# Early final norm in three places, old rows gathered ahead of both write-backs, last row scale on the sums

## Chip, cores and metric

One core of a Trainium2 chip runs the kernel. The metric is device time in microseconds (us) of one execution. The engines are TensorE (PE; its weight loads are PEld), VectorE (DVE), ScalarE (ACT), GpSimd (POOL) and SyncE (SP), whose queue issues most DMAs.

## What is computed

A layer over 2048 latent tokens of 1024 channels: a mixing sub-layer (convolution and mLSTM), then a channel sub-layer in which each of 16 experts picks its 256 tokens, then a final RMS norm. The change touches the end of this:

```python
def rmsnorm(x, g):
    xf = x.astype(jnp.float32)
    y = xf * lax.rsqrt(jnp.mean(xf * xf, axis=-1, keepdims=True) + EPS)
    return (y * g.astype(jnp.float32)).astype(x.dtype)

# one expert e: idx are its tokens, g their router weights
a = jnp.einsum('ecd,edf->ecf', xe, w_gate)
u = jnp.einsum('ecd,edf->ecf', xe, w_up)
ye = jnp.einsum('ecf,efd->ecd', jax.nn.silu(a) * u, w_down) * g[..., None]
...
xl = xl + ml[5] * expert_choice_moe(hl, w_router[layer], w_gate_e[layer], w_up_e[layer], w_down_e[layer])
return rmsnorm(xl, g_final)
```

ml[5] is a row of 1024 factors, the same for all tokens; in the kernel it is `ml5b`, and g_final is `gfb`.

## The kernel before

The experts run one after the other, e from 0 to 15. An expert's 1408 hidden channels are 11 tiles of 128, taken in six pairs (`pr` 0 to 5, the last with one tile). For each pair SP loads a tile of w_gate, of w_up (`load_w`, line 85) and of w_down (`wsplit_d`, line 1068). All products are made from a high and a low part: ScalarE copies the raw weights to the high part (line 92 `whi`, line 1074 `dhi`), VectorE subtracts it from the raw ones (line 96 `wlo`, line 1076 `dlo`). TensorE then does three matmuls for each product: lines 1173 to 1175 for gate and up (into `psx`), 1109 to 1111 for down (into four accumulators `ac`, two row halves by two column halves). The raw gate and up tiles have two buffers, their split parts three each, the w_down parts two.

After gate and up, ScalarE applies silu (1177), VectorE multiplies (1178), and the result is split again into `hh` (ScalarE, 1180) and `hl` (VectorE, 1182). The down product of a pair comes one pair later (`pend`), behind the gate and up matmuls of the next pair. When an expert's last pair is through, `finish` scales the sums by the token weight and ml5b (1128) and writes the rows to the tensor ACC in DRAM with an indirect DMA of GpSimd: experts 0 to 13 with an accumulating write (1133). Expert 14 gathers the old rows (1125), adds them (1131), writes (1135), norms the rows (squares, `rsqrt` on GpSimd in lines 80 and 81, lines 1138 and 1139) and scatters them to `out` (1140). Expert 15 does the same at the end (lines 1210 to 1231), but its w_down tiles have been multiplied by ml5b on GpSimd (line 1070), so that its sums need the token weight alone. 

In the last two experts the final norm of all 2048 rows is also computed early, in 16 tiles of 128 rows (`early`): load from ACC by SP (1092), square and row sum on ScalarE (1085), two small steps on GpSimd, scaling on VectorE (1095), store to `out` by SP (1096). Rows that experts 14 and 15 chose are overwritten by their scatters later. Expert 14 does two tiles in each pair from `pr` 1 on (tiles 0 to 9), expert 15 two in each of `pr` 1 to 3. Tiles with an even number use the buffer `ea` (one slot), the others `yv` (two slots), which the write-backs use too. The squares themselves are not needed; they go to a tile `eq` in the slot with the tag `oh`, of which there is one.

The rows of the next expert are fetched in `pr` 1 (`xgather`: a one-hot tile `oh` made by VectorE in line 1008, 16 matmuls into `pi`, line 1012, two gathers into the two slots `gx`, line 1018), and in `pr` 3 (`xprep`) TensorE transposes them (1052) and ScalarE and VectorE turn them into the high and low parts `xh` and `xl` (1055, 1060, 1061). The old rows of lines 1125 and 1213 use the slots `gx` as well.

The order on each engine and queue is set by a planner, which places each instruction when its inputs are there by its own estimate of times and takes what is earlier in the program first. On the chip every engine then runs its list in that order and waits where an input is not there.

Of the kernel before, what the change touches and what calls it, by code (L numbers as in the profile page):

```python
# [8 lines left out]
F32 = mybir.dt.float32  # L9
F32R = mybir.dt.float32r  # L10
BF16 = mybir.dt.bfloat16
I32 = mybir.dt.int32
I16 = mybir.dt.int16
AF = mybir.ActivationFunctionType
ALU = mybir.AluOpType
# [4 lines left out]
P = 128  # L20
# [18 lines left out]
def kernel(ctx, tc, x, c, cx, c_ctx, w_mod, b_mod, g_norm1, g_norm2, w_in, w_out, conv_w, conv_b,  # L39
# [956 lines left out]
    with tc.tile_pool(name="xw", bufs=2, reuse_waits="tile") as xraw, tc.tile_pool(name="xh", bufs=2, reuse_waits="tile") as xhi, \  # L996
# [67 lines left out]
        def wsplit_d(src, rows, gate=None, after=None, col=None):  # L1064
            raw = xraw.tile([P, rows, D], F32, name="draw", tag="draw")
            if gate is not None:
                V.tensor_copy(raw[:, 0, 0:1], gate)
            nc.sync.dma_start(raw, src)
            if col is not None:
                G.tensor_mul(raw, raw, col.unsqueeze(1).to_broadcast([P, rows, D]))  # L1070
            hi = xhi.tile([P, rows, D], F32R, name="dhi", tag="dhi")
            if after is not None:
                S.activation(hi[:, 0, 0:1], after, AF.Copy)
            S.activation(hi, raw, AF.Copy)  # L1074
            lo = xhi.tile([P, rows, D], F32R, name="dlo", tag="dlo")
            V.tensor_sub(lo, raw, hi.bitcast(F32))  # L1076
            return hi, lo
# [12 lines left out]
        def early(t):  # L1090
            a = wk.tile([P, D], F32, name="ea", tag="yv" if t % 2 else "ea", bufs=2 if t % 2 else 1)
            nc.sync.dma_start(a, ACC[t * P:(t + 1) * P, :])
            q = wk.tile([P, D], BF16, name="eq", tag="oh", bufs=1)
            fr = rms(a, q)
            V.scalar_tensor_tensor(a, a, fr, gfb, op0=ALU.mult, op1=ALU.mult)  # L1095
            nc.sync.dma_start(out[t * P:(t + 1) * P, :], a)
# [16 lines left out]
        def rows(e, hf_):  # L1113
            return bass.IndirectOffsetOnAxis(ap=idx_of[e][:, hf_:hf_ + 1], axis=0)

        idx_of = {}

        def finish(e, xp, accs, hfs=(0, 1)):
            gg = xp[2]
            idx_of[e] = xp[3]  # L1120
            for hf_ in hfs:
                yv = wk.tile([P, D], F32, name="yv", bufs=2)
                if e == NE - 2:
                    ar = wk.tile([P, XW], F32, name="gx", bufs=2)[:, :D]
                    G.indirect_dma_start(out=ar, out_offset=None, in_=ACC, in_offset=rows(e, hf_))
# [10 lines left out]
                q = wk.tile([P, D], BF16, name="eq", tag="oh", bufs=1)  # L1136
                fr = rms(yv, q)
# [5 lines left out]
        pend = []  # L1143
        for e in range(NE):
            xh, xl, gg, idx = xp
            accs = None
            nxt = None
            for pr in range(npair):
# [3 lines left out]
                for src in (w_gate_e, w_up_e):  # L1152
# [5 lines left out]
                    else:  # L1158
# [3 lines left out]
                              xl.bitcast(F32)[:, KD - 1, 0:1] if e == 0 and pr < 2 else None,  # L1162
                              ml5b if e == NE - 1 else None)
                if e == 0 and pr == 0:
                    other_places(xl.bitcast(F32)[:, KD - 1, 0:1])
                hts = []
# [17 lines left out]
                last = pr == npair - 1  # L1184
                if pend and not (e == NE - 1 and last):
# [9 lines left out]
                if e >= NE - 2 and pr:  # L1195
                    cuts = ((0, 2, 4, 6, 8, 10), (10, 12, 14, 16, 16, 16))[e - NE + 2]
                    for t in range(cuts[pr - 1], cuts[pr]):
                        early(t)
# [7 lines left out]
        idx_of[NE - 1] = xp[3]  # L1206
        with tc.manual_schedule(engines={mybir.EngineType.PE}):
            (_, _, _, p1, _), (_, _, _, p2, _) = pend
            order = [[(p1, 0, 0), (p1, 0, 1), (p2, 0, 0)], [(p2, 0, 1)], [(p1, 1, 0), (p1, 1, 1), (p2, 1, 0)], [(p2, 1, 1)]]
            for hf_ in range(2):  # L1210
# [3 lines left out]
                q = wk.tile([P, D], BF16, name="eq", tag="oh", bufs=1)  # L1214
                fs = wk.tile([P, 2], F32, name="fs2", bufs=2)
                fr = wk.tile([P, 2], F32, name="fr2", bufs=2)
                for cc in range(2):
                    sl = slice(cc * 512, (cc + 1) * 512)
                    for pp, h_, c_ in order[hf_ * 2 + cc]:
                        down(accs, pp, (h_,), (c_,))  # L1220
                    V.scalar_tensor_tensor(yv[:, sl], accs[hf_ * 2 + cc], xp[2][:, hf_:hf_ + 1], ar[:, sl],
                                           op0=ALU.mult, op1=ALU.add)
                    S.activation(q[:, sl], yv[:, sl], AF.Square, accum_out=fs[:, cc:cc + 1])
# [33 lines left out]
```

## Time and profile before

| | |
|---|---|
| time, median of 3 runs | 2733.11 us (2732.84 to 2739.49) |
| the profiled execution | 2732.62 us |
| its span, first to last instruction | 2730.7 us |
| busy: PE, DVE, ACT, POOL | 2635.4, 1598.7, 1153.0, 338.0 us |
| mean granted TensorE clock | 0.987 of full speed |
| moved by DMA | 524.58 MB, mean 192 GB/s |

The profile is of one execution. A matmul's start is as recorded and its end is modelled. In a list of waits, the arrow names what the waiting instruction was released by. In a timeline, the text in brackets is the idle time of the engine in front of the instruction and its releaser; merged instructions have a count (x2). The granted clock is given as a share of full speed.

### The profile page before, as it was taken

The numbers are of one execution on the slowest core, as the hardware profiler recorded it, in microseconds if no ns is written. First come the engines' busy times: TensorE is split into PE (matmuls) and PEld (weight loads), VectorE is DVE, ScalarE is ACT, GpSimd is POOL, SyncE is SP. The second block draws the span as 40 slices with busy tenths as digits, with TensorE's granted clock in tenths as the row PEclk, the third lists the DMA queues.
The fourth block names the chain that finished last, engine by engine and source line by source line (L and its number), as shares of the span: only waits on it lengthen the run. The fifth ranks groups of instructions, "written<-read, shape, count | busy, mean of one in ns | idle before, by whom it ended". The sixth has DMA issues, their size and how long they took to land. (4 is left out here: it accounts for less than half of the span.)

```text
span 2730.7 us, 42905 instructions
## 1 busy us (share of the span) xinstructions
PE 2635.4 (97%) x17569; PEld 2371.4 (87%) x17570; DVE 1598.7 (59%) x2566; ACT 1153.0 (42%) x1707; POOL 338.0 (12%) x351
## 2 busy tenths in 40 slices
PE   8999999999999999499999999999999999999988
PEld 4988888888878888389999999999999999999877
DVE  5356455553576665666556656655665665566585
ACT  3243333422534343354444444444444444444443
POOL 1010000000111111210011001101100110110353
PEclk9999999999999999799999999999999999999999
DMA  8444554545656564176666666666766675675865
GB/s 268 136 145 157 171 161 145 186 127 165 213 190 198 181 211 156 40 247 206 197 208 217 189 205 208 212 201 198 222 191 205 203 218 196 194 234 183 277 233 192
DMA packets 382533, 524.58 MB, mean 192 GB/s; under 512 B 15072, under 2 KB 322736, under 8 KB 380288
## 3 DMA queue, kind: packets, MB, share of 16 engines
q1 hardware_dynamic: 327968, 437.96, 49.8%
q10 hardware_dynamic: 43792, 46.55, 5.0%
q0 software_dynamic: 10576, 37.32, 4.9%
q8 instruction: 138, 2.26, 0.3%
q14 instruction: 59, 0.48, 0.1%
HBM read 449.05 MB, written 72.61 MB: 191 GB/s over the span
## 5 line engine op out<-in xcount | busy, mean ns | idle before, releaser
L1174 PE MATMUL psx<-xl,whi 128*128 128x256 f32 x2816 | 786.9, 280 | 4.0 <-DVE xl L1061 4.0
L1173 PE MATMUL psx<-xh,whi 128*128 128x256 f32 x2816 | 788.8, 281 | 1.4 <-ACT whi L92 1.4
L1175 PE MATMUL psx<-xh,wlo 128*128 128x256 f32 x2816 | 787.8, 280 | 0.6 <-DVE wlo L96 0.6
L96 DVE TENSOR_TENSOR wlo<-wraw,whi 128x2048 fp32r<-128x2048 f32 x248 | 539.8, 2187 | 308.1 <-ACT whi L92 305.0
L92 ACT ACTIVATE whi<-wraw 128x2048 fp32r<-128x2048 f32 x248 | 447.1, 1805 | 374.4 <-PE psx L1174 121.3
L1174 PEld LDWEIGHTS psx<-xl,whi 128*128 128x128 f32 x2816 | 530.7, 188 | 7.0 <-DVE xl L1061 4.6
L1173 PEld LDWEIGHTS psx<-xh,whi 128*128 128x128 f32 x2816 | 530.2, 189 | 4.3 <-ACT whi L92 1.6
L1175 PEld LDWEIGHTS psx<-xh,wlo 128*128 128x128 f32 x2816 | 530.7, 189 | 1.4 <-DVE wlo L96 1.3
L1111 PE MATMUL ac<-dhi,hl 128*128 128x512 f32 x704 | 277.7, 396 | 4.4 <-DVE hl L1182 4.4
L1109 PE MATMUL ac<-dhi,hh 128*128 128x512 f32 x704 | 280.3, 398 | 0.0
L1110 PE MATMUL ac<-dlo,hh 128*128 128x512 f32 x704 | 279.0, 396 | 0.0
L1076 DVE TENSOR_TENSOR dlo<-draw,dhi 128x2048 fp32r<-128x2048 f32 x96 | 202.9, 2113 | 115.1 <-ACT dhi L1074 115.1
L417 PE MATMUL ps<-hlo,whi 128*128 128x512 f32 (+1 forms) x672 | 259.9, 387 | 0.0
L418 PE MATMUL ps<-hhi,wlo 128*128 128x512 f32 (+1 forms) x672 | 259.6, 387 | 0.0
L416 PE MATMUL ps<-hhi,whi 128*128 128x512 f32 (+1 forms) x672 | 259.2, 388 | 0.0
L1133 POOL DMA_INDIRECT ACC<-yv,idx x28 | 82.8, 2958 | 1135.4 <-DVE yv L1128 1024.2
L1074 ACT ACTIVATE dhi<-draw 128x2048 fp32r<-128x2048 f32 x96 | 170.2, 1772 | 74.7 <-PE ac L1111 72.5
L1180 ACT ACTIVATE hh<-sgt 128x256 fp32r<-128x256 f32 x176 | 73.2, 417 | 276.2 <-DVE sgt L1178 276.2
L1111 PEld LDWEIGHTS ac<-dhi,hl 128*128 128x128 f32 x704 | 132.4, 188 | 36.4 <-DVE hl L1182 4.6
L1177 ACT ACTIVATE sgt<-psx 128x256 f32<-128x256 f32 x176 | 65.5, 373 | 230.3 <-PE psx L1175 230.2
L1110 PEld LDWEIGHTS ac<-dlo,hh 128*128 128x128 f32 x704 | 132.8, 189 | 26.9
L1109 PEld LDWEIGHTS ac<-dhi,hh 128*128 128x128 f32 x704 | 132.5, 188 | 27.1
(410 smaller groups left out, 3984.7 us busy)
## 6 DMA issues: line engine op xcount, KB each, us to landing
wraw<-in_w_gate_e_dram SPq DMA_DIRECT2D x80, 1024.0 KB, 7.3
wraw<-in_w_up_e_dram SPq DMA_DIRECT2D x80, 1024.0 KB, 5.5
draw<-in_w_down_e_dram SPq DMA_DIRECT2D x80, 1024.0 KB, 5.1
wraw<-in_w_in_dram SPq DMA_DIRECT2D x56, 1024.0 KB, 5.5
pk<-PK SPq DMA_DIRECT2D x16, 1284.0 KB, 7.0
xt<-in_x_dram SPq DMA_DIRECT2D x32, 512.0 KB, 4.9
wraw<-in_w_mod_dram SPq DMA_DIRECT2D x16, 1024.0 KB, 10.5
wm<-in_w_mod_dram SPq DMA_DIRECT2D x8, 1024.0 KB, 9.5
```

The lines of the kernel that those rows point to most:

```text
L92: S.activation(hi, raw, AF.Copy)
L96: V.tensor_sub(lo, raw, hi.bitcast(F32))
L416: T.matmul(ps[:, :ntok], wh, his[k], start=k == 0, stop=False)
L417: T.matmul(ps[:, :ntok], wh, los[k], start=False, stop=False)
L418: T.matmul(ps[:, :ntok], lo[:, k, i * P:(i + 1) * P], his[k], start=False, stop=k == KD - 1)
L1076: V.tensor_sub(lo, raw, hi.bitcast(F32))
L1109: T.matmul(ac, hhs, dh[:, i, sl], start=f == 0, stop=False)
L1110: T.matmul(ac, hhs, dl[:, i, sl], start=False, stop=False)
L1111: T.matmul(ac, hls, dh[:, i, sl], start=False, stop=f == NFT - 1)
L1173: T.matmul(ps[:, m_], wh, xh[:, k], start=k == 0, stop=False)
L1174: T.matmul(ps[:, m_], wh, xl[:, k], start=False, stop=False)
L1175: T.matmul(ps[:, m_], lo[:, k, i * P:(i + 1) * P], xh[:, k], start=False, stop=k == KD - 1)
```

## The change

- `early` is cut in three. `early_load` issues the load, now behind the weight loads of its pair and ahead of the pair's matmuls. `early_scale` does the square, row sum and GpSimd steps, behind the pair's last `hh`: a copy of one element of `hh` into the scrap tile ties it there. `early_store` does the scaling and the store, in the next pair behind its weight loads.
- The scrap output of the squares is a view of `ghb`, a constant whose contents aren't needed any more, and no longer a tile in the slot `oh`.
- The old rows of expert 14 are gathered for both halves in `old_rows`, at the end of its last pair; before, each half's gather stood in `finish`.
- For expert 15, the multiplication of w_down by ml5b is gone. The sums are scaled by the token weight and ml5b in one step, and the old rows are added in a second.

```diff
@@ -1061,13 +1061,11 @@
                     V.tensor_sub(xl[:, k], xf, xh.bitcast(F32)[:, k])
             return xh, xl, gg, idx
 
-        def wsplit_d(src, rows, gate=None, after=None, col=None):
+        def wsplit_d(src, rows, gate=None, after=None):
             raw = xraw.tile([P, rows, D], F32, name="draw", tag="draw")
             if gate is not None:
                 V.tensor_copy(raw[:, 0, 0:1], gate)
             nc.sync.dma_start(raw, src)
-            if col is not None:
-                G.tensor_mul(raw, raw, col.unsqueeze(1).to_broadcast([P, rows, D]))
             hi = xhi.tile([P, rows, D], F32R, name="dhi", tag="dhi")
             if after is not None:
                 S.activation(hi[:, 0, 0:1], after, AF.Copy)
@@ -1087,11 +1085,18 @@
             rsqrt(fr, fs, 1.0 / D, 1)
             return fr
 
-        def early(t):
+        sq = ghb.bitcast(BF16)
+
+        def early_load(t):
             a = wk.tile([P, D], F32, name="ea", tag="yv" if t % 2 else "ea", bufs=2 if t % 2 else 1)
             nc.sync.dma_start(a, ACC[t * P:(t + 1) * P, :])
-            q = wk.tile([P, D], BF16, name="eq", tag="oh", bufs=1)
-            fr = rms(a, q)
+            return [t, a]
+
+        def early_scale(rec, behind):
+            S.activation(sq[:, 0:1], behind, AF.Copy)
+            rec.append(rms(rec[1], sq))
+
+        def early_store(t, a, fr):
             V.scalar_tensor_tensor(a, a, fr, gfb, op0=ALU.mult, op1=ALU.mult)
             nc.sync.dma_start(out[t * P:(t + 1) * P, :], a)
 
@@ -1115,14 +1120,20 @@
 
         idx_of = {}
 
+        def old_rows(e):
+            for hf_ in range(2):
+                ar = wk.tile([P, XW], F32, name="gx", bufs=2)[:, :D]
+                G.indirect_dma_start(out=ar, out_offset=None, in_=ACC, in_offset=rows(e, hf_))
+                old.append(ar)
+
+        old = []
+
         def finish(e, xp, accs, hfs=(0, 1)):
             gg = xp[2]
-            idx_of[e] = xp[3]
             for hf_ in hfs:
                 yv = wk.tile([P, D], F32, name="yv", bufs=2)
                 if e == NE - 2:
-                    ar = wk.tile([P, XW], F32, name="gx", bufs=2)[:, :D]
-                    G.indirect_dma_start(out=ar, out_offset=None, in_=ACC, in_offset=rows(e, hf_))
+                    ar = old[hf_]
                 for cc in range(2):
                     sl = slice(cc * 512, (cc + 1) * 512)
                     V.scalar_tensor_tensor(yv[:, sl], accs[hf_ * 2 + cc], gg[:, hf_:hf_ + 1], ml5b[:, sl],
@@ -1133,16 +1144,16 @@
                     G.indirect_dma_start(out=ACC, out_offset=rows(e, hf_), in_=yv, in_offset=None, compute_op=ALU.add)
                     continue
                 G.indirect_dma_start(out=ACC, out_offset=rows(e, hf_), in_=yv, in_offset=None)
-                q = wk.tile([P, D], BF16, name="eq", tag="oh", bufs=1)
-                fr = rms(yv, q)
+                fr = rms(yv, sq)
                 V.tensor_mul(ar, yv, gfb)
                 V.tensor_scalar(ar, ar, fr, None, op0=ALU.mult)
                 G.indirect_dma_start(out=out, out_offset=rows(e, hf_), in_=ar, in_offset=None)
 
         xp = xprep(0, xgather(0))
-        pend = []
+        pend, held = [], []
         for e in range(NE):
             xh, xl, gg, idx = xp
+            idx_of[e] = idx
             accs = None
             nxt = None
             for pr in range(npair):
@@ -1159,10 +1170,15 @@
                         ws.append(split_w(raw, KD, n * P))
                 dw = wsplit_d(w_down_e[0, e][f0 * P:(f0 + n) * P, :].rearrange("(i p) n -> p i n", p=P), n,
                               gg[:, 0:1] if e == 0 and pr < 2 else None,
-                              xl.bitcast(F32)[:, KD - 1, 0:1] if e == 0 and pr < 2 else None,
-                              ml5b if e == NE - 1 else None)
+                              xl.bitcast(F32)[:, KD - 1, 0:1] if e == 0 and pr < 2 else None)
                 if e == 0 and pr == 0:
                     other_places(xl.bitcast(F32)[:, KD - 1, 0:1])
+                for rec in held:
+                    early_store(*rec)
+                held = []
+                if e >= NE - 2 and pr:
+                    cuts = ((0, 2, 4, 6, 8, 10), (10, 12, 14, 16, 16, 16))[e - NE + 2]
+                    held = [early_load(t) for t in range(cuts[pr - 1], cuts[pr])]
                 hts = []
                 for i in range(n):
                     ps = pmm.tile([P, 2, 2 * P], F32, name="psx", tag="mm")
@@ -1182,6 +1198,8 @@
                     V.tensor_sub(hl, sgt, hh.bitcast(F32))
                     hts.append((hh, hl))
                 last = pr == npair - 1
+                for rec in held:
+                    early_scale(rec, hts[-1][0].bitcast(F32)[:, 0:1])
                 if pend and not (e == NE - 1 and last):
                     pe, pxp, paccs, ppr, plast = pend.pop()
                     if paccs is None:
@@ -1192,10 +1210,8 @@
                     else:
                         accs = paccs
                 pend.append((e, xp, accs, ([f0 + i for i in range(n)], hts, dw), last))
-                if e >= NE - 2 and pr:
-                    cuts = ((0, 2, 4, 6, 8, 10), (10, 12, 14, 16, 16, 16))[e - NE + 2]
-                    for t in range(cuts[pr - 1], cuts[pr]):
-                        early(t)
+                if e == NE - 2 and last:
+                    old_rows(e)
                 if pr == 1 and e + 1 < NE:
                     gth = xgather(e + 1)
                 if pr == 3 and e + 1 < NE:
@@ -1203,7 +1219,6 @@
             if nxt is not None:
                 xp = nxt
         accs = pend[0][2]
-        idx_of[NE - 1] = xp[3]
         with tc.manual_schedule(engines={mybir.EngineType.PE}):
             (_, _, _, p1, _), (_, _, _, p2, _) = pend
             order = [[(p1, 0, 0), (p1, 0, 1), (p2, 0, 0)], [(p2, 0, 1)], [(p1, 1, 0), (p1, 1, 1), (p2, 1, 0)], [(p2, 1, 1)]]
@@ -1211,16 +1226,16 @@
                 yv = wk.tile([P, D], F32, name="yv", bufs=2)
                 ar = wk.tile([P, XW], F32, name="gx", bufs=2)[:, :D]
                 G.indirect_dma_start(out=ar, out_offset=None, in_=ACC, in_offset=rows(NE - 1, hf_))
-                q = wk.tile([P, D], BF16, name="eq", tag="oh", bufs=1)
                 fs = wk.tile([P, 2], F32, name="fs2", bufs=2)
                 fr = wk.tile([P, 2], F32, name="fr2", bufs=2)
                 for cc in range(2):
                     sl = slice(cc * 512, (cc + 1) * 512)
                     for pp, h_, c_ in order[hf_ * 2 + cc]:
                         down(accs, pp, (h_,), (c_,))
-                    V.scalar_tensor_tensor(yv[:, sl], accs[hf_ * 2 + cc], xp[2][:, hf_:hf_ + 1], ar[:, sl],
-                                           op0=ALU.mult, op1=ALU.add)
-                    S.activation(q[:, sl], yv[:, sl], AF.Square, accum_out=fs[:, cc:cc + 1])
+                    V.scalar_tensor_tensor(yv[:, sl], accs[hf_ * 2 + cc], xp[2][:, hf_:hf_ + 1], ml5b[:, sl],
+                                           op0=ALU.mult, op1=ALU.mult)
+                    V.tensor_add(yv[:, sl], yv[:, sl], ar[:, sl])
+                    S.activation(sq[:, sl], yv[:, sl], AF.Square, accum_out=fs[:, cc:cc + 1])
                     V.tensor_mul(ar[:, sl], yv[:, sl], gfb[:, sl])
                     G.tensor_scalar(fr[:, cc:cc + 1], fs[:, cc:cc + 1], 1.0 / D, fr[:, 0:1] if cc else EPS,
                                     op0=ALU.mult, op1=ALU.add)
```

## Rows read from the trace of the kernel before

**Rows 1.** Profile page, part 5: VectorE's split of line 96 over the whole span.

```profile
L96 DVE TENSOR_TENSOR wlo<-wraw,whi 128x2048 fp32r<-128x2048 f32 x248 | 539.8, 2187 | 308.1 <-ACT whi L92 305.0
```

**Rows 2.** Windows: us, busy us (instructions) per engine, TensorE clock, DMA share, GB/s.

```profile
2335.00:2431.00 96.00, 96.00 (x700) 89.69 (x700) 57.41 (x64) 44.55 (x49) 8.59 (x4) 1.00 0.65 206
2529.00:2626.00 97.00, 83.29 (x564) 76.98 (x563) 66.58 (x65) 44.38 (x59) 30.82 (x26) 0.95 0.80 276
2626.00:2731.00 105.00, 86.80 (x592) 79.31 (x591) 64.39 (x60) 41.41 (x61) 49.27 (x35) 0.94 0.56 191
```

**Rows 3.** Waits of TensorE, 2400 to 2735: us in total, times, longest.

```profile
PE pi L1012 <- DVE oh L1008: 5.4, 1, 5.4
PE ptx L1052 <- DVE xf L1060: 5.2, 1, 5.2
PE ac L1111 <- DVE hl L1182: 4.4, 1, 4.4
PE psx L1174 <- DVE xl L1061: 3.1, 1, 3.1
PE psx L1175 <- DVE wlo L96: 0.6, 2, 0.3
```

**Rows 4.** Windows right behind three of the waits, columns as before.

```profile
2543.85:2548.50 4.65, 4.65 (x25) 4.65 (x24) 3.79 (x5) 0.80 (x2) 1.12 (x2) 0.50 1.05 377
2601.13:2603.10 1.97, 1.97 (x11) 1.97 (x10) 1.23 (x1) 0.06 (x1) 0.00 (x0) 0.50 1.03 383
2646.82:2651.00 4.18, 4.18 (x11) 3.32 (x12) 2.70 (x3) 2.41 (x4) 1.19 (x2) 0.59 0.77 221
```

**Rows 5.** Timelines of VectorE and GpSimd: start, us, engine, line, operation [idle before].

```profile
2587.56 1.28 DVE L1095 SCALAR_TENSOR_TENSOR ea<-ea,fr,ml2b 128x1024 f32<-128x1024 f32 x1 [0.44 <-POOL fr L81]
...
2589.50 4.63 POOL L1070 TENSOR_TENSOR draw<-draw,ml5b 128x2048 f32<-128x2048 f32 x1
...
2589.56 5.65 DVE L1095 SCALAR_TENSOR_TENSOR ea<-ea,fr,ml2b 128x1024 f32<-128x1024 f32 x1 [0.72 <-POOL fr L81]
...
2608.98 6.49 POOL L1070 TENSOR_TENSOR draw<-draw,ml5b 128x2048 f32<-128x2048 f32 x1 [1.49 <-DVE ea L1095]
...
2611.39 6.23 DVE L96 TENSOR_TENSOR wlo<-wraw,whi 128x2048 fp32r<-128x2048 f32 x1
...
2638.83 5.07 DVE L1139 TENSOR_SCALAR gx<-gx,fr 128x1024 f32<-128x1024 f32 x1 [1.83 <-POOL fr L81]
...
2663.36 0.75 DVE L1139 TENSOR_SCALAR gx<-gx,fr 128x1024 f32<-128x1024 f32 x1 [1.47 <-POOL fr L81]
```

**Rows 6.** Timelines of ScalarE and VectorE around the first wait.

```profile
2538.24 1.06 ACT L1085 ACTIVATE eq<-ea 128x1024 bf16<-128x1024 f32 x1 [8.71 <-DMA ea<-ACC]
...
2540.70 0.40 ACT L1180 ACTIVATE hh<-sgt 128x256 fp32r<-128x256 f32 x1
...
2541.57 1.22 DVE L1008 TENSOR_TENSOR oh<-ix,UA 128x2048 bf16<-128x2048 bf16 x1
```

**Rows 7.** Timeline of SP's queue: issues of loads.

```profile
2522.13 0.37 SPq L1068 DMA_DIRECT2D draw<-in_w_down_e_dram  x1
2534.62 1.29 SPq L1092 DMA_DIRECT2D ea<-ACC  x3
2536.00 0.38 SPq L85 DMA_DIRECT2D wraw<-in_w_up_e_dram  x1
```

**Rows 8.** Timelines of GpSimd and VectorE: second half row write-back of expert 14.

```profile
2647.34 0.98 POOL L1125 DMA_INDIRECT gx<-ACC,idx  x1 [0.30 <-issue]
...
2656.92 1.29 DVE L1131 TENSOR_TENSOR yv<-yv,gx 128x512 f32<-128x512 f32 x2
```

**Rows 9.** Timelines of VectorE and ScalarE: second half, last expert.

```profile
2717.13 1.45 DVE L1221 SCALAR_TENSOR_TENSOR yv<-ac,gg,gx 128x512 f32<-128x512 f32 x2 [0.26 <-PE ac L1111]
...
2718.61 0.63 ACT L1223 ACTIVATE eq<-yv 128x512 bf16<-128x512 f32 x1
```

**Rows 10.** Page, part 6: issues, KB each, median us to landing.

```profile
wraw<-in_w_gate_e_dram SPq DMA_DIRECT2D x80, 1024.0 KB, 7.3
```

## What the change does to the time

> **What bounds the kernel now.** I read the stages first [rows 2]. A middle expert keeps TensorE busy for all of its 96.00 us at granted clock 1.00, so there nothing but matmul work counts, and the diff does not touch it. The last two experts hold the holes: 83.29 busy of 97.00 us and 86.80 of 105.00, at clocks 0.95 and 0.94. The DMA share is 0.80 and 0.56 there, so the transfers as a whole do not bound these stages, though single bursts may.
>
> Next, TensorE's own list of waits [rows 3]: five entries, 5.4, 5.2, 4.4, 3.1 and 0.6 us, together 18.7, and all of them end on VectorE. Idling has an after-cost: right after three of the waits the granted clock is 0.50, 0.50 and 0.59, that is at or near the lower level of 1.2 GHz, for 4.65, 1.97 and 4.18 us [rows 4]. At the upper level (2.4 GHz, clock 1.00) the work of these stretches takes 2.3, 1.0 and 1.7 us less, 5.0 in all. So 18.7 + 5.0 = 23.7 us is what the last two experts lose, and nearly all that a change here can win.
>
> Then who makes VectorE late. Three of the waits have one cause [rows 5]. At 2589.50 GpSimd starts its multiplication of a w_down tile (line 1070, 4.63 us); the row scaling of line 1095 that starts on VectorE at 2589.56 takes 5.65 us instead of 1.28 and ends just after it. The same holds for the split of line 96 at 2611.39, inside the 6.49 us of the next multiplication (6.23 instead of a mean of 2.19 [rows 1]), and for line 1139 at 2638.83 (5.07 instead of 0.75). The two engines did not share here: VectorE stood still until GpSimd was done.
>
> The first wait is of another kind [rows 6]. The one-hot tile of line 1008 is what TensorE waits for; it is written on VectorE only at 2541.57. Its buffer (tag "oh", one slot) also serves as scrap output of the early squares (line 1085), and ScalarE stood 8.71 us in front of the first of these until the rows of ACC had landed. That square and the next one also held up the copy to hh, which stood behind them until 2540.70. The rows were late because their load stood in SP's queue from 2522.5 to 2534.62, until the accumulating write of expert 13 had landed; the next weight load was issued at 2536.00 [rows 7].
>
> **Last row scale on the sums.** The six multiplications on GpSimd go away; what takes their place is one addition per row half and column half at the very end, and the scale moves into the step that reads the sums. What goes from the waits: 5.65 - 1.28 = 4.4 of the 5.2; 6.23 - 2.19 = 4.0, so all of the 3.1; 5.07 - 0.75 = 4.3 of the 4.4. Together 4.4 + 3.1 + 4.3 = 11.8, and with them the slow stretches behind the second and the fourth wait, 1.0 + 1.7 = 2.7. The sum is 14.5 us. Left are 0.8 + 0.1, and the 0.6 of the short waits I leave standing.
>
> The price is in the tail after the last matmul. An addition of 128x512 takes 1.29 / 2 = 0.64 us [rows 8]. At the end both multiply steps run back to back, and the square of the second half starts at 2718.61, when the second has ended [rows 9]; two additions get in between whatever their order, 1.28 us. The first row half shifts by the same, and VectorE had only 0.26 us to spare between the two halves [rows 9], so the other end of the bound is 1.28 + 1.28 - 0.26 = 2.3. I take the middle, 1.8 us.
>
> A rule of the Trainium skill bears on both. "SBUF — State Buffer", section "Who interferes with whom", says that an operation of VectorE with two inputs in SBUF and a GpSimd operation that reads SBUF exclude each other, and that whichever starts first holds the port for its whole length. The rows above agree. The rule also speaks against the change: the new additions have two inputs in SBUF, so VectorE would hold up GpSimd's small steps of the last norm; by it the tail would be up to another 0.64 us longer, and the sum below 2713.3.
>
> **Early final norm in three places.** The loads (16), squares and scalings are the same in number and size; added are 16 one-element copies on ScalarE, whose busy share here is under a half (44.38 of 97.00 us [rows 2]). I cost them at 16 x 0.2 = 3 us of an idle engine (estimate from the 1.06 us of a full square, between 0 and that), nothing on the path. If that cover is gone, they cost those 3 us. The scrap output now goes into a constant that is dead by then, so the one-hot tile needs to wait for nothing, and the square is tied behind the pair's last hh. The first wait should go, 5.4 us with its 2.3 of slow clock: 7.7 us. Bounds: 7.7, or nothing if VectorE is then taken by something else at 2537; I take 7.7, as rows 6 show VectorE free.
>
> What the ScalarE square is waiting for has not moved: the load of the early rows still waits in SP's queue for the ACC write. Behind it stand the weight loads of pair 3 and 4 of expert 14, and later those of expert 15. Their issue was 12.1 us late in the run before and no wait of TensorE ended on them, so I price this at nothing; with TensorE 7.7 us earlier, the margin is smaller by that, which is the first rival. The out stores move behind the next pair's weight loads in the program. In SP's queue that can only help the weights; who waits for a store is the next early load that needs its buffer (tags "ea", one slot, and "yv", two, which the write-backs use as well). ScalarE's squares wait for that load, and behind them stand weight splits and the evacuations of the next expert's rows.
>
> **Old rows gathered earlier.** Line 1125's second gather was issued at 2647.34, and the additions that need it ran only at 2656.92 [rows 8], some 30 us after the first half. Now both gathers stand at the end of expert 14. They need the two gx slots that the rows of expert 15 hold until their transposes are done; GpSimd's queue waits there, and behind it the small steps of the early norm. No wait of TensorE names this chain, so I cost it at nothing either way; bounds are zero and one wait like the smaller ones, 3.1. What it triggers is that the ACC write-back of expert 14 and the early loads behind it come some 30 us earlier, beside the weight loads of pairs 1 and 2.
>
> **The sum.** 14.5 + 7.7 - 1.8 = 20.4 us. The profiled execution took 2732.62 us (span 2730.7 and 1.9 around it), so 2712.2; the median of the three runs is 0.5 above that execution, which gives 2712.7. If all 23.7 come back and the tail costs 1.3, it is 2710.7; the restarts behind the waits, which I have not counted, may give 1 to 2 us more.
>
> **Rivals.** First, one new wait for weights or for the next expert's transposes, because TensorE now arrives earlier while SP still stands 12 us and ScalarE 8.7 us for early rows. Against it: the margin was there before. Its price is that of the wait of this size in the trace, 5.4 + 2.3 = 7.7: 2720.4 us. If it comes in both experts, 2728.1.
>
> Second, the change does not do all that it says, because the planner's order decides: the 5.2 and 3.1 us [rows 3] are waits of expert 15's transposes and for its xl. If that step stays late in the order, TensorE waits at the same places for ScalarE, and 4.4 + 3.1 + 1.0 = 8.5 us stay lost: 2721.2. With the first wait back as well (7.7) it is 2728.9.
>
> Third, the change turns slower: the early loads now stand in the program right behind the weights of their own pair, ahead of its matmuls. Should SP's queue follow that order, it would stand before the gate load of the next pair until the ACC write has landed. The price is at least the 12.1 us of the block [rows 7] and 2.3 of slow clock, and at most one landing of a weight tile more, 7.3 [rows 10]: 14.4 to 21.7 in each of the two experts, 36 in all, which gives 2749. It is slower than before from 10.2 us in each. Against it speaks that the queue is not in program order now: the w_down load at 2522.13 is the ninth from the last, so it belongs to pair 3 of expert 14 (pairs count from 0), and it stands ahead of the early loads of pair 1 [rows 7].
>
> **Chances.** Forecast (2709 to 2719): 0.62. One new wait, 2720: 0.16. Two, or waits that return, 2721 to 2729: 0.13, counted at its far end. Slower, 2749: 0.09. A measurement of this kernel can tell about 0.3%, 8.2 us, from no change; the first two cases are faster than that (0.78), the third I count within it, the fourth slower. The range reaches from 2708 (all of the loss and its restarts come back) to 2728 (both new waits).
>
> **What would show it.** Right: GpSimd has no operation over 4 us on w_down; no line 1095 or 96 on VectorE over 3 us; the pi matmuls start without a wait; TensorE busy nearly all of the time from 2529 on at clock 1.00, its last matmul some 22 us earlier; about 1.8 us more between it and the end. Wrong would be: TensorE waits that end on line 92 or a weight DMA, or on the transposes of line 1052; a tail over 2.5 us longer; SP standing much over 12 us before an early load.

## Result

The changed kernel takes 2711.3 us (median of 4 executions) where the kernel before takes 2733.35: a ratio of 0.992, 95% interval 0.9898 to 0.9941. The forecast was 2712.7, within 2708 to 2728. The profile after is of an execution of 2718.05 us (span 2716.3); the other three took 2711.95 and less, and a later part tells where most of the 7 us come from. One execution in all the runs below, of 6636.01 us in the kernel with the row scale and the early gathers, stands apart from the rest and is left out.

The first of the late stages in the profile after (columns as in [rows 2]):

```profile
2526.00:2621.00 95.00, 91.39 (x638) 84.74 (x637) 63.15 (x68) 52.69 (x74) 23.18 (x27) 0.96 0.90 304
```

A middle expert is as before (2335 to 2431: TensorE busy for all 96.00 us). The late window has 91.39 us of TensorE work in 95.00, where it had 83.29 in 97.00, and its clock is 0.96 for 0.95. The two windows are cut at fixed times and do not hold the same matmuls (638 and 564), so only their busy shares can be compared; the window behind holds the tail and can't be compared even so. Of the five waits of [rows 3] one name is left in the list of TensorE's waits, at another size and place:

```profile
PE ptx L1052 <- DVE xf L1060: 3.6, 1, 3.6
```

It stands before the second group of transposes of expert 15's rows, not before the third. The chain of work that ended last, given in shares of the span, says the same in another way: now TensorE makes 64%, in the lines of the matmuls, and GpSimd 0%. Before, the chain could be followed only through a few per cent of the span, with GpSimd at 1% and TensorE at 0%. The chains before and after:

```profile
issue 2%; POOL 1%; DMA 1%; DVE 1%; PE 0%; ACT 0%; POOLq 0%; DVEq 0%; SPq 0%
...
PE 64%; DMA 2%; issue 2%; DVE 2%; ACT 0%; POOL 0%; POOLq 0%; DVEq 0%; ACTq 0%; SPq 0%
```

The tail grew by 1.75 us, where 1.8 had been forecast. From the start of the second half's sums to the last scatter's issue it was 2721.88 - 2717.13 = 4.75 us before (start in [rows 9]); after, it is 2707.55 - 2701.05 = 6.50. The timelines of VectorE and GpSimd:

```profile
2701.05 0.75 DVE L1235 SCALAR_TENSOR_TENSOR yv<-ac,gg,ml5b 128x512 f32<-128x512 f32 x1 [0.35 <-PE ac L1116]
2701.72 0.48 DVE L1244 TENSOR_SCALAR gx<-gx,fr 128x512 f32<-128x512 f32 x1
...
2702.77 1.28 DVE L1237 TENSOR_TENSOR yv<-yv,gx 128x512 f32<-128x512 f32 x2
...
2707.55 1.06 POOL L1246 DMA_INDIRECT out_dram<-gx,idx  x1 [1.50 <-ACT gx L1245]
```

### The profile page after: what moved, and what is told of

Read it like the earlier page. It is cut to its first block, busy times and chain, and to the rows that moved or that the text cites. A ratio compares the mean times of both kernels' runs of the same rounds, so it can differ in the third digit from the quotient of the medians.

```text
span 2716.3 us, 42922 instructions
## 1 busy us (share of the span) xinstructions
PE 2633.9 (97%) x17570; PEld 2371.2 (87%) x17570; DVE 1582.9 (58%) x2570; ACT 1156.8 (43%) x1723; POOL 303.7 (11%) x345
## 4 chain that ended last, share of the span: by engine, by line
PE 64%; DMA 2%; issue 2%; DVE 2%; ACT 0%; POOL 0%; POOLq 0%; DVEq 0%; ACTq 0%; SPq 0%
PE psx L1189 11%; PE psx L1190 11%; PE psx L1191 11%; PE ac L1114 6%; PE ac L1115 6%; PE ac L1116 6%; PE po L729 2%; PE po L730 2%; PE po L731 2%; DMA pk<-PK 1%; PE pb L513 1%; PE ptx L1052 1%; PE pl L765 1%; PE pa L509 1%; DVE jk L929 1%
## 5 line engine op out<-in xcount | busy, mean ns | idle before, releaser
L96 DVE TENSOR_TENSOR wlo<-wraw,whi 128x2048 fp32r<-128x2048 f32 x248 | 531.3, 2153 | 314.4 <-ACT whi L92 311.3
## 6 DMA issues: line engine op xcount, KB each, us to landing
wm<-in_w_mod_dram SPq DMA_DIRECT2D x8, 1024.0 KB, 11.4
```

## Which wait went with which part

Seven kernels do or undo parts. The first four do one part alone on the kernel before; their expectations were written from the same terms as the prediction.

**The row scale alone.**

```diff
-                              xl.bitcast(F32)[:, KD - 1, 0:1] if e == 0 and pr < 2 else None,
-                              ml5b if e == NE - 1 else None)
+                              xl.bitcast(F32)[:, KD - 1, 0:1] if e == 0 and pr < 2 else None)
...
-                    V.scalar_tensor_tensor(yv[:, sl], accs[hf_ * 2 + cc], xp[2][:, hf_:hf_ + 1], ar[:, sl],
-                                           op0=ALU.mult, op1=ALU.add)
+                    V.scalar_tensor_tensor(yv[:, sl], accs[hf_ * 2 + cc], xp[2][:, hf_:hf_ + 1], ml5b[:, sl],
+                                           op0=ALU.mult, op1=ALU.mult)
+                    V.tensor_add(yv[:, sl], yv[:, sl], ar[:, sl])
```

> The kernel before with the last row scale on the sums and nothing else of the change. Theory (each wait has its own cause): the 5.2, 4.4 and 3.1 us waits shrink to under 1 us together with their slow clock (14.5), the 5.4 us wait for the one-hot tile stays, the tail grows by 1.3 to 2.3: about 2720.7 us. Rival (the early squares in front of hh and of the transposes are the deeper cause): the waits come back with ScalarE in VectorE's place, gain under 5 us: 2728 or more.

Measured: 2724.82 us against 2734.75 of the kernel before on the same chip, ratio 0.9969 (0.9956 to 0.9981): 9.9 us, where 12.7 were expected. TensorE's waits:

```profile
PE pi L1012 <- DVE oh L1008: 5.8, 1, 5.8
PE ac L1111 <- DVE hl L1181: 2.3, 1, 2.3
PE ptx L1052 <- DVE xf L1060: 2.1, 2, 1.7
PE psx L1173 <- DVE xl L1061: 0.3, 1, 0.3
```

The waits that stood behind GpSimd's multiplication fell from 5.2, 4.4 and 3.1 to 2.1, 2.3 and 0.3, not to 0.8, 0.1 and nothing. The wait for the one-hot tile stayed (5.8). The mechanism holds, its size was put 4 us too high: what VectorE gets back, TensorE does not get in full. The trace shows what holds the rest of the wait for hl: VectorE stands before the second addition of the old rows, and the hl at 2640.75 is behind it.

```profile
2639.54 1.29 DVE L1131 TENSOR_TENSOR yv<-yv,gx 128x512 f32<-128x512 f32 x2 [7.12 <-DMA gx<-ACC,idx]
```

So that wait had a second cause, which the early gathers take away. In front of the transposes it is an early square again: ScalarE waited 4.17 us for its rows until 2588.21, and hh, the scalings and the splits came behind it.

**The scrap output alone.**

```diff
+        sq = ghb.bitcast(BF16)
...
-            q = wk.tile([P, D], BF16, name="eq", tag="oh", bufs=1)
-            fr = rms(a, q)
+            fr = rms(a, sq)
```

(and the same for the two write-backs)

> The kernel before with the squares' scrap output moved out of the slot of the one-hot tile, nothing else. Theory: the 5.4 us wait of the pi matmuls and the 2.3 us of slow clock behind it go: 2725.7 us, the other three waits stay as they are. Rival (the slot is only the last thing to come late; hh behind the squares holds the next down product at the same place): a wait of several us at another line between 2533 and 2560, no gain: 2733.

Measured: 2734.55 us against 2734.75, ratio 0.9999 (0.999 to 1.0008). Nothing. The wait for the one-hot tile is gone and the time with it is not won:

```profile
PE ptx L1052 <- DVE xf L1060: 11.8, 2, 8.8
PE psx L1173 <- ACT whi L92: 2.6, 1, 2.6
PE psx L1174 <- DVE xl L1061: 1.8, 1, 1.8
PE psx L1175 <- DVE wlo L96: 1.4, 1, 1.4
```

The transposes now wait 11.8 us instead of 5.2, and two entries, 2.6 and 1.4 us, stand on weights. The timelines of ScalarE, VectorE and GpSimd ahead of the longest of these waits (2599.4 to 2608.45) show whose time it is:

```profile
2593.33 1.06 ACT L1085 ACTIVATE ghb<-ea 128x1024 bf16<-128x1024 f32 x1 [5.34 <-DMA ea<-ACC]
...
2594.82 0.43 DVE L1182 TENSOR_TENSOR hl<-sgt,hh 128x256 fp32r<-128x256 f32 x1 [5.73 <-ACT hh L1180]
...
2597.70 5.57 DVE L1096 SCALAR_TENSOR_TENSOR ea<-ea,fr,ml2b 128x1024 f32<-128x1024 f32 x1 [0.72 <-POOL fr L81]
...
2597.63 4.56 POOL L1070 TENSOR_TENSOR draw<-draw,ml5b 128x2048 f32<-128x2048 f32 x1
...
2607.77 0.54 DVE L1060 TENSOR_SCALAR xf<-ptx,A,B 128x256 f32<-128x256 f32 x1
```

ScalarE stands 5.34 us before an early square whose rows have not landed, the hh behind it comes at 2594.39, VectorE has been idle for 5.73 us by then; the scaling that follows is locked out by GpSimd's multiplication (5.57 instead of 1.28), and the evacuation that the transposes need ends at 2608.3. None of these rows is released by TensorE. Counted from expert 14's first matmul, TensorE came to this wait 2.8 us earlier than before (two waits of 1.4 and 3.0 us in front of it had taken the rest) and left it 0.7 us later: it stood longer at the next door. All its waits together are 17.6 us, where they were 18.7.

**The early norm in three places alone** (with the scrap output, without the row scale and the early gathers).

```diff
-                    for t in range(cuts[pr - 1], cuts[pr]):
-                        early(t)
+                    held = [early_load(t) for t in range(cuts[pr - 1], cuts[pr])]
...
+                for rec in held:
+                    early_store(*rec)
...
+                for rec in held:
+                    early_scale(rec, hts[-1][0].bitcast(F32)[:, 0:1])
```

> Early norm in three places and the scrap output out of the slot, but with the multiplications on GpSimd and the old rows' gathers as before. Theory: 7.7 us as with the scrap output alone, the three waits that the multiplications make stay: 2725.7 us. Rival (splitting the early norm also takes its work out of the way of the multiplications and of the transposes): over 12 us of gain, 2721 or less.

Measured: 2723.74 us against 2734.75, ratio 0.9963 (0.9949 to 0.9976): 11.0 us where I had 7.7. TensorE's two longest waits (three more are under 2 us):

```profile
PE ptx L1052 <- DVE xf L1060: 3.6, 1, 3.6
PE psx L1194 <- DVE xl L1061: 3.2, 1, 3.2
```

The difference to the scrap output alone is the order: the loads stand ahead of the pair's matmuls, the squares behind hh and the scalings one pair later. What the runs say, then, is that the 7.7 us were not to be had by freeing the slot; they were to be had by taking the early work out from between TensorE's results and the next transposes. Whether the order alone would do it, with the scrap output left in the slot, was not tried.

**The old rows gathered early, alone.**

```diff
-                    ar = wk.tile([P, XW], F32, name="gx", bufs=2)[:, :D]
-                    G.indirect_dma_start(out=ar, out_offset=None, in_=ACC, in_offset=rows(e, hf_))
+                    ar = old[hf_]
...
+                if e == NE - 2 and last:
+                    old_rows(e)
```

> Only the old rows of expert 14 gathered for both halves at the end of its last pair. Theory: the write-back of expert 14 comes about 30 us earlier, and no wait of TensorE goes or comes: 2733.4 us, within 3. Rival (the late second half is behind the 4.4 us wait for hl): that wait goes and 4 to 6 us with it: 2728.

Measured: 2734.79 us against 2734.75, ratio 1.0004 (0.9995 to 1.0013). Two of TensorE's four waits (the others are those for the one-hot tile and for xl, as before):

```profile
PE ptx L1052 <- DVE xf L1060: 5.7, 1, 5.7
PE psx L1181 <- DVE sgt L1186: 5.6, 1, 5.6
```

The 4.4 us wait for hl is gone, so the rival had the mechanism; a wait of 5.6 us for sgt stands there instead, so the theory had the time.

**The changed kernel without the early gathers.** The diff is that of the part before, undone.

> The changed kernel with the old rows of expert 14 gathered one by one in the write-back, as before. Theory: the early gathers are worth nothing on TensorE's path: 2711, within 2. Rival (with the other waits gone the late second half of the write-back is what comes late next, and holds the early loads of expert 15 and weights behind them): 2715 or more, with a wait of TensorE after 2615.

Measured: 2720.49 us, ratio to the kernel before 0.9954 (0.994 to 0.9967). The changed kernel, beside it on the same chip, took 2715.15. So the part that is worth nothing alone is worth 5.3 us here. The longest of TensorE's waits, and the timelines of GpSimd and VectorE that explain it:

```profile
PE ac L1116 <- DVE hl L1199: 3.7, 1, 3.7
```

```profile
2627.49 1.55 POOL L1137 DMA_INDIRECT gx<-ACC,idx  x1 [7.36 <-DMA ACC<-yv,idx]
...
2635.42 1.29 DVE L1143 TENSOR_TENSOR yv<-yv,gx 128x512 f32<-128x512 f32 x2 [6.96 <-DMA gx<-ACC,idx]
...
2636.63 0.42 DVE L1199 TENSOR_TENSOR hl<-sgt,hh 128x256 fp32r<-128x256 f32 x1
```

The second gather waits 7.36 us in GpSimd's queue for the write of the first half to land; both name the tensor ACC. VectorE, which executes in its order, stands 6.96 us before the addition that needs it, and the hl that TensorE wants stands behind it. In the changed kernel both gathers are issued ahead of the first write; the timeline of GpSimd:

```profile
2604.81 2.26 POOL L1126 DMA_INDIRECT gx<-ACC,idx  x1 [4.70 <-PE ptx L1052]
2607.38 0.95 POOL L1126 DMA_INDIRECT gx<-ACC,idx  x1 [0.30 <-issue]
2617.82 3.00 POOL L1146 DMA_INDIRECT ACC<-yv,idx  x1 [4.22 <-DVE yv L1142]
```

**The changed kernel with GpSimd's multiplication put back.** The diff is the first one, undone.

> The changed kernel with the multiplication of w_down on GpSimd and the old last row scale put back (early norm in three places and early gathers stay). Theory (waits add up, each with its own cause): the row scale is worth what it gave alone, 9.9 us; 2725 where the changed kernel takes 2715. Rival (the waits follow one another, and what one part frees the next takes up): its worth here differs by over 3 us from what it gave alone.

Measured: 2723.31 us, ratio to before 0.9965 (0.9952 to 0.9977), where the changed kernel took 2711.94 beside it on the same chip: the row scale is worth 11.4 us here, 9.9 alone. That is a difference of 1.5 us, as the theory had it, but 3.3 of the 11.4 lie ahead of expert 14 (its first matmul starts at 2503.73 here and at 2500.43 in the profile beside it), and the table below speaks for the rival. The lock is back on VectorE's timeline, on a pair of additions that takes 1.29 us undisturbed [rows 8]:

```profile
2630.75 4.68 POOL L1070 TENSOR_TENSOR draw<-draw,ml5b 128x2048 f32<-128x2048 f32 x1
...
2630.28 5.71 DVE L1144 TENSOR_TENSOR yv<-yv,gx 128x512 f32<-128x512 f32 x2
```

**The row scale and the early gathers without the early norm in three places.** Both diffs are shown above.

> The kernel before with the last row scale on the sums and the early gathers, the early norm as before. Theory A (the early gathers count only once TensorE gets to the write-back of expert 14 early, which needs the early norm split too): as the row scale alone, 2724. Theory B (they count as soon as the multiplications are gone from GpSimd's queue, where the second gather stood behind them): the wait for hl after 2635 goes too, 2720 or less.

Measured: 2720.27 us (five executions), ratio to before 0.9954 (0.9941 to 0.9967). That is 12.3 us against 9.9 for the row scale alone: nearer to theory B by its number, but the two differ by 2.4 us only and were not run side by side. One of TensorE's waits:

```profile
PE psx L1180 <- DVE sgt L1185: 1.1, 1, 1.1
```

The wait for hl is gone (2.3 with the row scale alone), which is what theory B named; one of 1.1 us stands instead. The 5.7 us for the one-hot tile is what the missing part leaves.

Against the kernel before, run beside them on the same chip, in us. The second column is read from one profile each: it compares the stretch from the first gate matmul of expert 14 to the end, which was 228.7 us before (2502.01 to 2730.67) and holds all that the change touches. In every profile expert 13 in front of it takes 95.3 us. Three profiles of the changed kernel differ by 1.9 us in it.

| parts | time won | won in the stretch |
|---|---|---|
| row scale | 9.9 | 9.4 |
| early norm in three places | 11.0 | 9.6 |
| old rows early | 0.0 | -1.0 |
| row scale, early norm | 12.5 | 11.4 |
| early norm, old rows | 9.2 | 11.2 |
| row scale, old rows | 12.3 | 11.5 |
| all three (three measurements) | 22.1, 17.8, 20.6 | 17.1, 17.5, 19.0 |

In the stretch each pair wins some 11.4 us, whichever part is missing, and the third part adds 5.6 to 7.7 more. So the parts do not add up: 9.4 and 9.6 give 11.4 together, and a part that wins nothing alone wins as much as the others when it comes last. I read this as waits in series: each part takes away one place at which VectorE comes late between 2535 and 2650, and as long as one of them is left, it takes up a part of what the others free. The scrap output alone shows it directly, by the wait that grew; it won 0.7 us in the stretch.

## What is left

**The changed kernel twice more.** The first profile had a wait of 3.6 us and a time 7 us above the other executions.

> The changed kernel once more, for a second profile. The profiled execution of the first look took 2718.05 us and had one TensorE wait of 3.6 us at the transposes plus some 3 us of slow clock; the other three took 2711. Theory A: that wait is missing in the usual execution, which explains the 7 us: time 2711, a profile at 2711 has no TensorE wait over 1 us. Theory B: the wait is in every execution and the 7 us came from the stages before expert 14: then the profile has the wait at any time.

> The changed kernel as the measure for the other three of this chip: 2711 to 2715 us, with the one wait at the transposes of 2.8 to 3.6 us.

Measured: 2715.15 us (ratio 0.9933, 0.9919 to 0.9946) and 2711.94 us (0.9924, 0.9911 to 0.9937). The wait is in each of them, in the order of the two kernels, so theory B is right:

```profile
PE ptx L1052 <- DVE xf L1060: 2.8, 1, 2.8
```

```profile
PE ptx L1052 <- DVE xf L1060: 3.0, 1, 3.0
```

What differs is when the one-hot matmuls (line 1012) that fetch expert 15's rows come up on TensorE. TensorE's timelines of the first profile and of the last one:

```profile
2535.57 1.15 PE L1012 MATMUL pi<-Cb,oh 128*128 128x4 bf16 x16
```

```profile
2531.24 1.15 PE L1012 MATMUL pi<-Cb,oh 128*128 128x4 bf16 x16
```

The matmuls stand 4.33 us apart, and everything ahead of them is the same program. The same 4.33 us are there at the first matmul of expert 14 (2504.76 and 2500.43) and already at that of expert 4 (1552.20 and 1547.87). So of the 6.2 us between the two spans (2716.3 and 2710.1) 4.3 come from the stages ahead of the change; they are no matter of this change, and the gain is best read from the stretch behind them, or between kernels run side by side.

**Where the last wait comes from.** The timeline of VectorE in the first profile:

```profile
2576.70 1.29 DVE L1100 SCALAR_TENSOR_TENSOR ea<-ea,fr,ml2b 128x1024 f32<-128x1024 f32 x1 [1.96 <-POOL fr L81]
...
2578.71 1.28 DVE L1100 SCALAR_TENSOR_TENSOR ea<-ea,fr,ml2b 128x1024 f32<-128x1024 f32 x1 [0.72 <-POOL fr L81]
...
2579.91 2.28 DVE L1074 TENSOR_TENSOR dlo<-draw,dhi 128x2048 fp32r<-128x2048 f32 x1
...
2583.36 0.53 DVE L1060 TENSOR_SCALAR xf<-ptx,A,B 128x256 f32<-128x256 f32 x1
```

A group of transposes is evacuated in two steps of line 1060; the second is the one shown, and the next group, which uses the same buffer, starts at 2584.04 after 3.61 us of waiting. The two scalings of pair 3 and a w_down split stand in front of both steps. They are behind the next pair's weights in the program, but the planner puts them where it thinks VectorE free.

> The changed kernel with the early tiles dealt out differently: none in pair 3 of expert 14, where the next expert's rows are transposed, the others one pair later (the last two in pair 4 of expert 15). Theory: the two squares and two scalings of that pair stand in front of the evacuation of the first transposes on ScalarE and VectorE and cause the left-over wait of 3.6 us and its slow clock: that wait goes, 2711 less up to 6.7 us, at best 2705. Rival (the transposes are late for another reason, or the wait moves to the following pair): 2711 or more.

```diff
-                    cuts = ((0, 2, 4, 6, 8, 10), (10, 12, 14, 16, 16, 16))[e - NE + 2]
+                    cuts = ((0, 2, 4, 4, 6, 8), (8, 10, 12, 14, 16, 16))[e - NE + 2]
```

Measured: 2711.85 us against 2715.15 of the changed kernel beside it (ratio to before 0.9923, 0.991 to 0.9937): 3.3 us. The wait at the transposes shrinks to 0.4, so the cause is the one named, and a new one comes at the very end:

```profile
PE ac L1114 <- ACT hh L1196: 2.1, 1, 2.1
PE ptx L1052 <- DVE xf L1060: 0.4, 1, 0.4
```

There the last two scalings (the second is shown) stand in front of the last sgt and hh; the timeline of VectorE:

```profile
2686.16 1.29 DVE L1100 SCALAR_TENSOR_TENSOR ea<-ea,fr,ml2b 128x1024 f32<-128x1024 f32 x1 [0.72 <-POOL fr L81]
...
2688.50 0.42 DVE L1194 TENSOR_TENSOR sgt<-psx,sgt 128x256 f32<-128x256 f32 x1
```

> The changed kernel with the early tiles dealt as 3, 3, 0, 2, 2 over the pairs of expert 14 and 2, 2, 2 over those of expert 15 (the buffer goes by the place in the pair). Theory: no early work beside the first transposes, so the wait of 2.8 to 3.6 us there and the slow clock behind it go, and no square stands before the last hh: 3 to 6 us below the changed kernel on this chip. Rival (three tiles in a pair block SP's queue or ScalarE for longer): no gain, with a wait of TensorE between 2545 and 2575.

```diff
-            a = wk.tile([P, D], F32, name="ea", tag="yv" if t % 2 else "ea", bufs=2 if t % 2 else 1)
+            a = wk.tile([P, D], F32, name="ea", tag="yv" if i else "ea", bufs=2 if i else 1)
...
-                    cuts = ((0, 2, 4, 6, 8, 10), (10, 12, 14, 16, 16, 16))[e - NE + 2]
+                    cuts = ((0, 3, 6, 6, 8, 10), (10, 12, 14, 16, 16, 16))[e - NE + 2]
```

Measured: 2714.86 us against 2711.94 of the changed kernel beside it (ratio to before 0.9933, 0.9921 to 0.9946). No gain, and the wait at the transposes is back at 2.9 us. It is not where the rival had put it, so both expectations missed. The timeline of VectorE:

```profile
2568.78 1.28 DVE L1100 SCALAR_TENSOR_TENSOR ea<-ea,fr,ml2b 128x1024 f32<-128x1024 f32 x1 [0.71 <-POOL fr L81]
...
2571.12 0.42 DVE L1194 TENSOR_TENSOR sgt<-psx,sgt 128x256 f32<-128x256 f32 x1
```

The third scaling of pair 2 and a weight split stand in front of this sgt. Counted from expert 14's first matmul it comes 2.46 us later than in the deal before (2571.12 - 2500.63 against 2569.67 - 2501.64), and the wait is longer by as much (2.89 against 0.42). Behind the sgt come hh, the split of w_down and then the evacuation. So the early work had moved from one place in front of the evacuation to another; that is read from the trace, no run tried it.

The first deal is a little better than the changed kernel: each of its five executions is faster than each of the five beside it, and its stretch from expert 14 on takes 208.4 us, where the three profiles of the changed kernel have 209.7 to 211.6. The second deal's 210.2 us lie among these.

**The tail.**

> The changed kernel without the four additions of the old rows at the very end (its output lacks the old rows of expert 15's tokens). Theory: the additions lengthen the way from the last matmul to the end by 1.3 to 2.3 us: 2709.5. Rival (the row scale's GpSimd steps or the scatter end last anyway): no change, 2711.

```diff
-                    V.tensor_add(yv[:, sl], yv[:, sl], ar[:, sl])
                     S.activation(sq[:, sl], yv[:, sl], AF.Square, accum_out=fs[:, cc:cc + 1])
```

Measured: 2711.35 us against 2715.15 of the changed kernel beside it (ratio to before 0.9923, 0.9909 to 0.9936). From the start of the second half's sums to the last scatter it takes 2701.81 - 2697.07 = 4.74 us, 1.76 less than with the additions. The timelines of VectorE and GpSimd:

```profile
2697.07 1.45 DVE L1235 SCALAR_TENSOR_TENSOR yv<-ac,gg,ml5b 128x512 f32<-128x512 f32 x2 [0.27 <-PE ac L1116]
...
2701.81 1.06 POOL L1245 DMA_INDIRECT out_dram<-gx,idx  x1 [1.32 <-ACT gx L1244]
```

The other 2 us of the difference do not lie in the tail. Between the two profiles (2714.2 and 2710.6 us), 0.7 us lie ahead of expert 14 and 1.1 us between its first matmul and the last one, where the three profiles of the changed kernel differ by 1.9 us among themselves.

## Why the prediction was right, and where it was not

**The time.** Forecast 20.4 us, measured 22.1, and 17.8 and 20.6 when measured again; in the stretch from expert 14 on it is 17.1 to 19.0. What held is the reading that the change clears the way for nearly all of TensorE's waits behind that point: they fell from 18.7 us to 3.6, 2.8 and 3.0, where 1.5 were to be left. What did not hold is the adding up. Of the terms only the tail was right; the row scale was put too high, the early norm had the wrong reason and the old rows were put at nothing, and that these errors went against each other is luck. So are, by these stretches, some 3 of the 22.1 us: they lie ahead of the change.

**The row scale, 14.5 us in the waits and 1.8 in the tail.** Right in mechanism: VectorE's operations of 5 us and more are gone in the profile after and come back with GpSimd's multiplication. The waits were over-sized: alone the net was 9.9 instead of 12.7; undone in the changed kernel it was 11.4, of which 5.9 to 7.7 lie in the stretch. The step that failed is "5.65 - 1.28 = 4.4 of the 5.2": it takes the time that an operation was too long for the time that TensorE was too late. An early square held the transposes as well, and the late old rows held hl. The tail was right at 1.75, the middle of the bounds by some luck: 1.28 us are the two additions, and 0.4 come from the first half's last scaling (line 1244), which now runs between the two sums and ran ahead of them before. VectorE was not late for the second half, as the upper bound had it; it was idle for 0.35 us before its first sum. The extra 0.64 us that the prediction gave by the Trainium skill ("SBUF — State Buffer", "Who interferes with whom") did not come, and this run does not test it: the additions had ended at 2704.05, before the first of GpSimd's two steps (line 1240). These took 0.25 and 0.32 us beside VectorE's multiplications, where their counterparts (line 1225) took 0.44 and 0.39 before:

```profile
2704.46 0.25 POOL L1240 TENSOR_SCALAR fr<-fs 128x1 f32<-128x1 f32 x1
2705.07 0.32 POOL L1240 TENSOR_SCALAR fr<-fs,fr 128x1 f32<-128x1 f32 x1 [0.36 <-ACT ghb L1238]
```

**The early norm, 7.7 us.** The size came out near (11.0 alone, 8.3 where the other two are there: 2720.27 - 2711.94), the reason was wrong. The step was "the one-hot tile needs to wait for nothing ... 7.7 us": that was the slot, and freeing the slot gave nothing. What gave the time is the order: hh no longer stands behind a square that waits for a transfer, and the scalings come later; the runs do not tell these two apart. The copies that tie the squares to hh took 0.2 us each, as estimated. In the profile after, ScalarE still waits 5.38 us for the early rows, but hh has passed at 2534.71; the timeline of ScalarE:

```profile
2534.71 0.42 ACT L1196 ACTIVATE hh<-sgt 128x256 fp32r<-128x256 f32 x1 [2.42 <-DVE sgt L1194]
...
2543.06 1.06 ACT L1083 ACTIVATE ghb<-ea 128x1024 bf16<-128x1024 f32 x1 [5.38 <-DMA ea<-ACC]
```

My prediction named that square and hh behind it, and then priced the part by the wait that the list of TensorE showed instead.

**The old rows, nothing.** Wrong: 5.3 us in the changed kernel, beyond my bound of 3.1. "No wait of TensorE names this chain" was true of the trace before, where another wait covered it, and alone the part is indeed worth nothing. The row that should have warned me is in [rows 8]: an addition 30 us behind its time on an engine that executes in order. In the row scale alone the wait for hl stands behind just this addition.

**SP's queue.** I priced its 12 us at nothing, and this held: it stood from 2525.25 (2524.88 + 0.37) to 2538.07 for the early rows, 12.8 us, the next weights were issued at 2539.45, and no wait of TensorE ends on weights. The slower rival (the loads ahead of the next gate tile in SP's order) did not come: w_down's tile of pair 3 still stands ahead of them. SP's queue in the profile after:

```profile
2524.88 0.37 SPq L1068 DMA_DIRECT2D draw<-in_w_down_e_dram  x1
2538.07 1.29 SPq L1092 DMA_DIRECT2D ea<-ACC  x3
2539.45 0.62 SPq L85 DMA_DIRECT2D wraw<-in_w_up_e_dram  x1
```

**The rivals.** One wait did come at the transposes, as the first rival had it, but with 2.8 to 3.6 us instead of 5.4. Its place is the second rival's (the evacuation still late in the order), but it ends on VectorE and not on ScalarE. In the first profile the granted clock behind it is 0.54 from 2584.00 to 2590.00, which makes 6.00 x 0.46 = 2.8 us; with the 3.6 it costs 6.4 us, where the forecast had left 0.8.

## What to carry over

A list of an engine's waits says what came last, not what it is worth to remove it: where other engines run in a fixed order, the next late step takes the time, and no pair of parts was worth more than 12.5 us where the three gave some 20 (in the stretch from expert 14 on, 11.5 and 17 to 19). Before such small gains are compared, the stages ahead of the change have to be taken out. So before a wait is priced, follow the in-order engine behind it up to the next thing that TensorE takes from it, and ask what stands there and what that is waiting for. An operation that waits for a transfer belongs behind everything that the main chain needs from its engine; moving it (with the loads ahead of it and the scalings that follow it) gave 11 us where freeing its buffer gave nothing.

## What was not expected of the chip

The same program ahead of the change came up to 4.33 us earlier or later at the same matmul (2535.57 and 2531.24), a fifth of the gain that was to be measured; all of it had arisen before expert 4. And in this program the gather from ACC waited 7.36 us in GpSimd's queue for the landing of the write to ACC ahead of it, and VectorE then stood 6.96 us for the gathered rows.
